# Attention transposes in three groups under a pinned TensorE order, the last token group of layer 1 issued later, and one norm pass on ScalarE

## The chip, the cores and the metric

The kernel runs on one core of one Trainium2 chip. The metric is the device time of one execution in microseconds (us). Engines are named as the profile names them: PE is TensorE's matmul stream and PEld its weight loads, DVE is VectorE, ACT is ScalarE, POOL is GpSimd, SP is SyncE. The program holds one list of instructions for each engine, and engines wait for each other by semaphores.

## The reference

One inference step of a two-layer backbone over 128 context tokens and 1024 latent tokens, width 1024, all in float32. Layer 0 mixes tokens by chunkwise retention and pooling, layer 1 by attention; each is followed by a SwiGLU FFN, with RMS norms around every part and a shift and scale from a conditioning vector. Cut to what the change touches:

```python
def rmsnorm(x, gain):
    y = x32 * lax.rsqrt(jnp.mean(x32 * x32, axis=-1, keepdims=True) + EPS)
    return y.astype(x.dtype) * gain

# attention of the latent tokens: 8 heads, 2 key/value heads, head dimension 128,
# keys: 256 cached and 1024 latent ones
s = jnp.einsum('bqkgd,btkd->bkgqt', qblk, k).astype(jnp.float32) * scale
p = jax.nn.softmax(s, axis=-1).astype(v.dtype)
return jnp.einsum('bkgqt,btkd->bqkgd', p, v)

xs = xs + g2s * rmsnorm(fs, norm_gain[i, 3])              # end of layer i
hs = rmsnorm(xs, norm_gain[i, 0]) * (1.0 + sc1s) + sh1s   # start of the next
```

## The kernel before, in words

All nine token tiles of 128 (tile 0 is the context, 1 to 8 the latent tokens) stay in SBUF. A float32 product is made of three passes in a faster 32-bit format: `split` writes the high half of a tile by a ScalarE cast (L156) and the low half by a VectorE subtraction (L157), and `mm3` (L179) multiplies high by high, high by low and low by high.

**Order of the work.** The kernel is traced in Python. A scheduler then sets the order on each engine by its own estimate of when each instruction is ready; the order of the Python program is its priority, not its law. Two calls bind it: `keep_in_program_order` ties an instruction behind the one traced before it on its engine, and `issue_after` puts a block behind a named instruction. In the kernel before, TensorE's attention work is bound by neither. The framework sets the semaphores, one for each pair of instructions that touch the same data.

**Attention** (L1256 to L1362) goes over 32 pairs n, each of one latent token tile and two heads (e = 0 and 1).
- `q_split` (L1256 on) splits the queries of pair n on GpSimd.
- `scores(n, e)` multiplies 128 queries by 1280 keys into PSUM columns 1280·e to 1280·e+1280 in three pieces of 512, 512 and 256 columns, each of three matmuls. The kernel counts PSUM in banks of 512 columns (`bank`), so that both heads' quarter pieces of 256 lie in bank 2: columns 1024 to 1280 are head 0's last piece, 1280 to 1536 are head 1's first. Then come the row maximum over 1280 columns on VectorE (L1271), the exponential with its sum on ScalarE (L1273), the reciprocal (L1274), and the scaling by it, on ScalarE for e = 0 (L1278) and on VectorE for e = 1 (L1276).
- `p_trans(n, u)`, written T, makes four 128x128 transposes on TensorE (L1289), two key blocks of both heads, into PSUM bank 5 or 6, and splits the result (L156, L157).
- `values(n, u)`, written V, multiplies two key blocks of the values by the transposed probabilities: six matmuls of 256 columns, summed over u = 0 to 4 in bank 7. After u = 4 ScalarE copies the result out (L1307).

The order of a pair is written as a string (L1343): T, V and v stand for `p_trans` and `values` of pair n and of the pair before, S0 and S1 for `scores` of the next pair. At eight of the pairs a block of `w_o` is loaded and split as well (L1356 to L1359).

**From layer 0 to layer 1.** The FFN's output stage of layer 0 (`output`) ends every token tile with `chain_steps`: a gated norm (L220 to L234), the residual sum stored to DRAM (L235), the sum of squares on ScalarE (L237), its power -1/2 on GpSimd (L184, L185), and the normalised tile (L240, VectorE). When three tiles are through, `hsteps` queues eight steps in the list `later`; each makes three transposes (L255), shift and scale on ScalarE (L258), and the high and low half on VectorE (L260, L261). `go(n)` issues the next n of them. The projection of layer 1 runs `qkv_step` for blocks bi = 0 and 1 over token groups g = 0, 1, 2 of three tiles, 24 matmuls each, with calls of `go` between.

Of the kernel before, what the change touches and what calls it, by code (L numbers as in the profile page):

```python
# [64 lines left out]
def hybrid_step_kernel(ctx: ExitStack, tc: tile.TileContext, a: dict, outs: list):  # L65
# [45 lines left out]
    def bank(i, n=1):  # L111
        return PS[:, i * 512:(i + n) * 512]
# [25 lines left out]
    def tok(t):  # L138
        return O[:, :, t * 128:(t + 1) * 128]
# [28 lines left out]
    def load_pair(src, hl):  # L168
        hi, lo = hl
        for s in range(2):  # L170
            load_unit(src[:, 4 * s:4 * s + 4], (hi[:, 4 * s:4 * s + 4].rearrange("p k f -> p (k f)"),
                                               lo[:, 4 * s:4 * s + 4].rearrange("p k f -> p (k f)")), k=4)

    def mm3(out, items, first=True, last=True):
        n = 3 * len(items)
        c = 0
        for lh, ll, rh, rl in items:
            for x, y in ((lh, rh), (lh, rl), (ll, rh)):
                nc.tensor.matmul(out=out, lhsT=x, rhs=y, start=(first and c == 0), stop=(last and c == n - 1))  # L179
                c += 1  # L180

    def rstd_of(ss, n, w=1):
# [23 lines left out]
    def load_gates(l, s):  # L206
        for k in range(2):
            nc.sync.dma_start(out=GB[k], in_=g_scr[l][s][k][0:1, :].broadcast_to([128, D]))

    def chain_steps(t, src, xs, xd, junk, last=False):  # L210
        if last:
            xb = (XB + [RAW[:, 0], RAW[:, 1]])[t % 4]
        else:
            xb = XB[t] if t < 2 else (XB[0], GB[0], XB[1])[(t - 2) % 3]
        nc.sync.dma_start(out=xb, in_=xs)
        ot = tok(t)
        ss = sm()
        if len(src.shape) == 2:
            src = src.rearrange("p (k f) -> p k f", k=KD)
        nc.scalar.activation(junk, src, ACTF.Square, accum_out=ss)  # L220
        r = rstd_of(ss, D)
        yield
        g = GB[0 if t == 0 else 1].rearrange("p (k f) -> p k f", k=KD)
        x3 = xb.rearrange("p (k f) -> p k f", k=KD)
        if last:
            n = 2 if t == 8 else 1
            for i in range(n):
                c = slice(i * KD // n, (i + 1) * KD // n)
                nc.vector.scalar_tensor_tensor(ot[:, c], src[:, c], r, g[:, c], op0=ALU.mult, op1=ALU.mult)  # L229
                nc.vector.tensor_add(x3[:, c], ot[:, c], x3[:, c])  # L230
                nc.sync.dma_start(out=xd.rearrange("t (k f) -> t k f", k=KD)[:, c], in_=x3[:, c])
            return
        nc.vector.scalar_tensor_tensor(ot, src, r, g, op0=ALU.mult, op1=ALU.mult)
        nc.vector.tensor_add(x3, ot, x3)  # L234
        nc.gpsimd.dma_start(out=xd, in_=xb)  # L235
        s2 = sm()
        nc.scalar.activation(ot, x3, ACTF.Square, accum_out=s2)  # L237
        r2 = rstd_of(s2, D)
        yield
        nc.vector.tensor_scalar(ot, x3, r2, None, op0=ALU.mult)  # L240

    def chain(*args, **kw):
        for _ in chain_steps(*args, **kw):
# [21 lines left out]
    def go(n=99):  # L265
        for _ in range(min(n, len(later))):
            later.pop(0)()
# [497 lines left out]
    class FFN:  # L765
# [241 lines left out]
        def output(self):  # L1007
            l = self.l
            last_layer = self.next_sub is None
            self.S2 = open_mid2(F32)  # L1010
            self.out_load(3)
            self.out_load(4)
            if l == 0:
                nc.gpsimd.memset(XGT[:, 2048:3072], 0.0)
                adaq.append(Ada(1, 2, ada_bufs(XGT[:, 0:4096]), 4))
            f0, nb = 0, 0
            live = []

            def advance():
                for item in list(live):  # L1020
                    t, g = item
                    if next(g, None) is None and g.gi_frame is None:
                        live.remove(item)
                        if not last_layer and t % 3 == 2:
                            hsteps(t // 3, self.next_sub, (6, 7) if t < 8 else (4, 5), t == 8)

            for ci, nf in enumerate(NCH):
                fs = range(f0, f0 + nf)
                f0 += nf
                todo = list(range(f0, f0 + NCH[ci + 1])) if ci + 1 < len(NCH) else []  # L1030
                start = 6 if ci == 0 else 3
                every = (18 - start) // len(todo) if todo else 99
                lastc = ci == len(NCH) - 1
                if lastc:
                    load_gates(l, 1)
                    if not last_layer:
                        load_blk(0)
                for t in range(NT):
                    js = slice(t * 128, t * 128 + 128)
                    for half in range(2):  # L1040
                        ps = bank(nb % 4)
                        items = []
                        for f in fs:
                            gh, gl, wh, wl = self.out_slot(f)
                            items.append((gh[:, js], gl[:, js], wh[half], wl[half]))
                        mm3(ps, items)
                        dst = O[:, 4 * half:4 * half + 4, js]
                        p3 = ps.rearrange("p (k f) -> p k f", k=4)
                        if ci == 0:
                            nc.scalar.copy(dst, p3)  # L1050
                        else:
                            nc.vector.tensor_add(dst, p3, dst)  # L1052
                        nb += 1
                        n = 2 * t + half
                        if todo and n >= start and (n - start) % every == 0:
                            f = todo.pop(0)
                            self.out_split(f)
                            if f + 3 < NF:
                                self.out_load(f + 3)
                        if not lastc and ci > 0 and n % 4 == 3:  # L1060
                            hook()
                        go(2)
                    if lastc:
                        advance()
                        junk = PS[:, 2048:3072].rearrange("p (k f) -> p k f", k=KD)
                        g = chain_steps(t, tok(t), self.xs(t), self.xd(t), junk, last=last_layer)
                        next(g)
                        live.append((t, g))
            while live:
                advance()  # L1070
                if not last_layer and live and live[-1][0] == 8:
                    go()
            if not last_layer:
                load_blk(1)
# [181 lines left out]
    def q_split(n):  # L1256
        t, hp = pairs[n]
        qh, ql = qsb[n % 2]
        src = O[:, 2 * hp:2 * hp + 2, t * 128:(t + 1) * 128]
        nc.gpsimd.tensor_copy(qh, src)  # L1260
        nc.gpsimd.tensor_sub(ql, src, qh)
# [19 lines left out]
    pts = {}  # L1281

    def p_trans(n, u):
        tp = bank(5 + u % 2)
        for jj in range(2):
            for e in range(2):
                c = (2 * jj + e) * 128
                j = 2 * u + jj
                nc.tensor.transpose(tp[:, c:c + 128], smx[n, e][:, j * 128:(j + 1) * 128], ident)  # L1289
        b = RR[:, 1024 * (st["u"] % 6):1024 * (st["u"] % 6) + 1024]  # L1290
        st["u"] += 1
        split(b[:, 0:512], b[:, 512:1024], tp)
        pts[n, u] = b
# [15 lines left out]
    for g in range(NG):  # L1309
        for bi in range(2):  # L1310
            for t in range(3 * g, 3 * g + 3):
                qkv_step(bi, t)
                go(2 if (g, bi) > (0, 0) else 0)
        go()
    load_blk(2)
    load_blk(3)
    side = {(3, 2): cached_k, (5, 1): cached_v}
# [19 lines left out]
        f()  # L1337

    q_split(1)
    for n in range(len(pairs)):  # L1340
        if n + 2 < len(pairs):
            q_split(n + 2)
        for w in 'T0 v3 S0 T1 v4 T2 S1 T3 V0 V1 T4 V2'.split():  # L1343
            c, u = w[0], int(w[1])
            if c == 'S' and n + 1 < len(pairs):
                scores(n + 1, u)
            elif c == 'T':
                p_trans(n, u)
            elif c == 'V':
                values(n, u)  # L1350
            elif c == 'v' and n:
                values(n - 1, u)
        if n % 2 == 1 and 6 <= n // 2 < 14:
            k = n // 2 - 6
            r = raw()
            nc.sync.dma_start(out=r, in_=a["w_o"][0, k * 128:(k + 1) * 128, :])  # L1356
            with tc.issue_after(st["act"].ins if hasattr(st["act"], "ins") else st["act"]):
                nc.scalar.copy(units[k][0], r)
            nc.vector.tensor_sub(units[k][1], r, units[k][0])  # L1359

    values(len(pairs) - 1, 3)
    values(len(pairs) - 1, 4)  # L1362
    load_gates(1, 0)
    F = FFN(1, M1, lambda t: x_scr[2][t], x_out, None)
    out_proj(F, units, [0, 1, 2, 3, 4, 5, 6, 7], [0, 1, 2, 3, 4], lambda t: [(tok(t), 0, 8)],
# [31 lines left out]
```

## Time and profile before

| | |
|---|---|
| median of 3 runs | 2904.22 us (2900.73 to 2904.52) |
| the profiled execution's own time | 2904.19 us |
| its span, first to last instruction | 2902.4 us |
| PE busy | 2835.7 us, 98% of the span |
| DVE, ACT, POOL busy | 1796.5, 1044.0, 299.8 us |
| mean granted TensorE clock | 0.994 |
| attention, first to last transpose (L1289) | 1699.6 to 2003.5 us |

The page of the profile lists busy time by engine, the span in 40 slices, the queues, the chain that ended last and the costliest groups of instructions. A row of the timeline reads: start and length in us, engine, line, operation, tile written <- tiles read, shapes, count of instructions merged, and in brackets the engine's idle time before it and what ended it. In attention the tiles tell the steps apart: `PS<-CT,XGT` at L1289 are transposes; `PS<-MID1True,RR` at L179 are scores (keys in MID1True), 128x512 for the large pieces and 128x256 for the quarter pieces; `PS<-RR` and `PS<-RR,MID2True` are values. The table by windows gives busy us of each engine, the count of instructions in brackets, and PEclk, the granted share of the TensorE clock.

### The profile page before, as it was taken

The numbers are of one execution on the slowest core, as the hardware profiler recorded it, in microseconds if no ns is written. First come the engines' busy times: TensorE is split into PE (matmuls) and PEld (weight loads), VectorE is DVE, ScalarE is ACT, GpSimd is POOL, SyncE is SP. The second block draws the span as 40 slices with busy tenths as digits, with TensorE's granted clock in tenths as the row PEclk, the third lists the DMA queues.
The fourth block names the chain that finished last, engine by engine and source line by source line (L and its number), as shares of the span: only waits on it lengthen the run. The fifth ranks groups of instructions, "written<-read, shape, count | busy, mean of one in ns | idle before, by whom it ended". The sixth has DMA issues, their size and how long they took to land. (4 is left out here: it accounts for less than half of the span.)

```text
span 2902.4 us, 44728 instructions
## 1 busy us (share of the span) xinstructions
PE 2835.7 (98%) x17979; PEld 2554.2 (88%) x17979; DVE 1796.5 (62%) x3019; ACT 1044.0 (36%) x1950; POOL 299.8 (10%) x542
## 2 busy tenths in 40 slices
PE   7999999999999999999999999999999999999998
PEld 4889998788999999977779988888889999998886
DVE  5784455526767676665775667786486555554455
ACT  5222222426223223331243457785362222234111
POOL 2010111111000000000033621110100000000000
PEclk9999999999999999999999999999999999999999
DMA  7541110412333333353331000001223222225222
GB/s 247 163 122 52 36 34 26 141 65 73 105 114 120 112 126 99 129 167 115 122 132 62 23 16 1 23 30 59 91 81 111 72 73 77 76 74 180 78 92 102
DMA packets 194056, 262.59 MB, mean 90 GB/s; under 512 B 10220, under 2 KB 139688, under 8 KB 193720
## 3 DMA queue, kind: packets, MB, share of 16 engines
q1 hardware_dynamic: 182272, 217.88, 23.8%
q0 software_dynamic: 11088, 41.47, 3.8%
q8 instruction: 141, 2.31, 0.3%
q14 instruction: 67, 0.55, 0.1%
q10 hardware_dynamic: 488, 0.38, 0.0%
HBM read 213.52 MB, written 46.17 MB: 89 GB/s over the span
## 5 line engine op out<-in xcount | busy, mean ns | idle before, releaser
L179 PE MATMUL PS<-RR 128*128 128x256 f32 (+2 forms) x6270 | 1134.9, 333 | 1.3 <-ACT O L1050 0.7
L179 PEld LDWEIGHTS PS<-RR 128*128 128x128 f32 x6270 | 959.9, 190 | 117.6 <-issue 19.0
L843 PE MATMUL PS<-RR 128*128 128x288 f32 x5324 | 734.2, 297 | 12.9 <-ACT RR L156 7.0
L843 PEld LDWEIGHTS PS<-RR 128*128 128x128 f32 x5324 | 717.0, 189 | 24.2 <-ACT RR L156 7.9
L156 ACT CAST RR<-O 128x512 fp32r<-128x512 f32 (+1 forms) x242 | 151.8, 628 | 535.1 <-PE PS L843 468.7
L179 PE MATMUL PS<-RR,MID2True 128*128 128x256 f32 (+1 forms) x1416 | 269.2, 338 | 0.2 <-ACT RR L156 0.2
L1052 DVE TENSOR_TENSOR O<-PS,O 128x512 f32<-128x512 f32 x216 | 148.9, 689 | 172.8 <-PE PS L179 172.0
L179 PEld LDWEIGHTS PS<-RR,MID2True 128*128 128x128 f32 x1416 | 218.2, 189 | 30.5 <-ACT RR L156 0.8
L157 DVE TENSOR_TENSOR RR<-O,RR 128x512 fp32r<-128x512 f32 (+1 forms) x242 | 167.5, 693 | 72.4 <-ACT RR L156 72.4
L157 DVE TENSOR_TENSOR RR<-RAW,RR 128x512 fp32r<-128x512 f32 (+1 forms) x119 | 110.2, 932 | 101.8 <-ACT RR L156 78.7
L345 DVE SCALAR_TENSOR_TENSOR O<-O,PW 128x512 f32<-128x512 f32 x224 | 159.7, 745 | 18.4 <-ACT O L343 9.4
L156 ACT CAST RR<-RAW 128x512 fp32r<-128x512 f32 (+1 forms) x119 | 95.4, 808 | 207.4 <-PE PS L843 92.4
L179 PE MATMUL PS<-MID1True,RR 128*128 128x512 f32 (+1 forms) x630 | 166.7, 372 | 2.2 <-ACT XGT L1273 1.7
L843 PE MATMUL PS<-MID1True,RR 128*128 128x288 f32 x1100 | 159.9, 295 | 0.0
L843 PEld LDWEIGHTS PS<-MID1True,RR 128*128 128x128 f32 x1100 | 150.9, 189 | 0.0
L843 PE MATMUL PS<-MID2True,RR 128*128 128x288 f32 x968 | 147.0, 295 | 0.0
L184 POOL TENSOR_SCALAR SM<-SM 128x1 f32<-128x1 f32 (+1 forms) x153 | 56.6, 370 | 793.0 <-ACT PS L220 304.8
L843 PEld LDWEIGHTS PS<-MID2True,RR 128*128 128x128 f32 x968 | 135.5, 189 | 0.0
L874 POOL DMA_DIRECT2D gg<-XGT x44 | 23.6, 537 | 961.5 <-DVE XGT L873 961.5
L1271 DVE TENSOR_REDUCE SM<-PS 128x1 f32<-128x1280 f32 x64 | 95.5, 1491 | 40.5 <-PE PS L179 40.0
L179 PEld LDWEIGHTS PS<-MID1True,RR 128*128 128x128 f32 x630 | 102.7, 189 | 17.7 <-ACT XGT L1273 2.6
L156 ACT CAST RR<-PS 128x512 fp32r<-128x512 f32 x160 | 93.7, 587 | 64.6 <-PE PS L1289 63.5
(292 smaller groups left out, 3091.0 us busy)
## 6 DMA issues: line engine op xcount, KB each, us to landing
O<-in_w_ada_dram SPq DMA_DIRECT2D x64, 512.0 KB
RAW<-in_w_ffn_in_dram SPq DMA_DIRECT2D x100, 256.0 KB
gg<-XGT POOLq DMA_DIRECT2D x44, 576.0 KB, 3.1
O<-in_w_ffn_in_dram SPq DMA_DIRECT2D x92, 256.0 KB
RAW<-in_w_ffn_out_dram SPq DMA_DIRECT2D x30, 512.0 KB
MID2False<-gg SPq DMA_DIRECT2D x26, 576.0 KB
RAW<-in_w_in_even_dram SPq DMA_DIRECT2D x28, 512.0 KB
x<-XGT POOLq DMA_DIRECT2D x27, 512.0 KB, 3.2
```

What stands on the lines that cost most here:

```text
L156: nc.scalar.copy(hi, src)
L157: nc.vector.tensor_sub(lo, src, hi)
L179: nc.tensor.matmul(out=out, lhsT=x, rhs=y, start=(first and c == 0), stop=(last and c == n - 1))
L184: nc.gpsimd.tensor_scalar(r, ss, 1.0 / n, EPS, op0=ALU.mult, op1=ALU.add)
L345: nc.vector.scalar_tensor_tensor(self.acc[kind], b[:, k], sv, self.acc[kind], op0=ALU.mult, op1=ALU.add)
L843: nc.tensor.matmul(out=ps, lhsT=u[:, ks], rhs=v, start=first and n == 0, stop=n == 11, skip_group_check=not first)
L874: nc.gpsimd.dma_start(out=gg_scr[self.l][f], in_=XGT[:, 2880:4032])
L1052: nc.vector.tensor_add(dst, p3, dst)
L1271: nc.vector.reduce_max(nm, sp, axis=AX.X, negate=True)
```

## The change

Three edits.

1. **Attention order.** The string becomes `T0 T1 v3 S0 v4 S1 T2 T3 V0 V1 T4 V2`, so that a pair's five transpose steps stand in groups of two, two and one. From the first pair to the end of the last, every TensorE instruction of `mm3` and `p_trans` is bound to the program's order by `keep_in_program_order`. The bank of `p_trans` alternates over all steps, not within a pair.
2. **Last token group of layer 1.** The eight steps of group g = 2, which wait in `later` when the projection begins, are issued from g = 1 on, not within g = 0.
3. **Norm pass.** In the FFN's output stage of layer 0 the last step of `chain_steps` (the normalised tile, nine times) runs on ScalarE.

```diff
+    pin = {"pe": False}
+
+    def pe(ins):
+        return tc.keep_in_program_order(ins) if pin["pe"] else ins
...
-                nc.tensor.matmul(out=out, lhsT=x, rhs=y, start=(first and c == 0), stop=(last and c == n - 1))
+                pe(nc.tensor.matmul(out=out, lhsT=x, rhs=y, start=(first and c == 0), stop=(last and c == n - 1)))
...
-        nc.vector.tensor_scalar(ot, x3, r2, None, op0=ALU.mult)
+        if act:
+            nc.scalar.activation(ot, x3, ACTF.Identity, scale=r2)
+        else:
+            nc.vector.tensor_scalar(ot, x3, r2, None, op0=ALU.mult)
...
-                        g = chain_steps(t, tok(t), self.xs(t), self.xd(t), junk, last=last_layer)
+                        g = chain_steps(t, tok(t), self.xs(t), self.xd(t), junk, last=last_layer, act=True)
...
     def p_trans(n, u):
-        tp = bank(5 + u % 2)
+        tp = bank(5 + st["u"] % 2)
...
-                nc.tensor.transpose(tp[:, c:c + 128], smx[n, e][:, j * 128:(j + 1) * 128], ident)
+                pe(nc.tensor.transpose(tp[:, c:c + 128], smx[n, e][:, j * 128:(j + 1) * 128], ident))
...
-                go(2 if (g, bi) > (0, 0) else 0)
-        go()
+                go(2 if g else 0)
+        if g:
+            go()
...
     q_split(1)
+    pin["pe"] = True
...
-        for w in 'T0 v3 S0 T1 v4 T2 S1 T3 V0 V1 T4 V2'.split():
+        for w in 'T0 T1 v3 S0 v4 S1 T2 T3 V0 V1 T4 V2'.split():
...
     values(len(pairs) - 1, 4)
+    pin["pe"] = False
```

More of the change, by code (lines that the diff above doesn't have):

```diff
@@ L208, in load_gates, with chain_steps @@
             nc.sync.dma_start(out=GB[k], in_=g_scr[l][s][k][0:1, :].broadcast_to([128, D]))
-    def chain_steps(t, src, xs, xd, junk, last=False):
+    def chain_steps(t, src, xs, xd, junk, last=False, act=False):
         if last:
```

## The prediction

> **What bounds the kernel now.** I read the page first, then the timeline of one attention pair by engine, then the granted clock by windows, and last the passage from layer 0 to layer 1.
>
> ```profile
> span 2902.4 us, 44728 instructions
> ## 1 busy us (share of the span) xinstructions
> PE 2835.7 (98%) x17979; PEld 2554.2 (88%) x17979; DVE 1796.5 (62%) x3019; ACT 1044.0 (36%) x1950; POOL 299.8 (10%) x542
> ```
>
> TensorE is busy for 98% of 2902.4 us. Whatever makes it idle is paid in full, and whatever another engine saves is worth nothing unless TensorE was waiting for it. So I ask of each edit only where TensorE will stand still. Most depends on the 32 attention pairs. One of them on TensorE:
>
> ```profile
> 1856.43 0.61 PE L179 MATMUL PS<-MID1True,RR 128*128 128x256 f32 x3
> 1856.87 0.60 PE L1289 MATMUL PS<-CT,XGT 128*128 128x128 f32 x4
> 1857.23 0.95 PE L179 MATMUL PS<-RR,MID2True 128*128 128x256 f32 x6
> 1858.02 1.55 PE L179 MATMUL PS<-MID1True,RR 128*128 128x512 f32 x6
> 1859.41 0.73 PE L1289 MATMUL PS<-CT,XGT 128*128 128x128 f32 x5
> 1860.07 0.62 PE L179 MATMUL PS<-MID1True,RR 128*128 128x256 f32 x3
> ```
>
> Lengths overlap, since matmuls are pipelined, so I take differences of starts. A transpose step and a values step together need 1858.02 - 1856.87 = 1.15 us. Six large score matmuls need 1859.41 - 1858.02 = 1.39. A matmul of 256 columns needs 0.12 (47 of them stand at 5.88 us in a row below), so a values step is 0.72, a transpose step 0.43, and three quarter-piece matmuls 0.36. A head's scores are 1.39 + 0.36 = 1.75. A pair is 5 x 1.15 + 2 x 1.75 = 9.25 us of TensorE. The same pair on VectorE and on ScalarE:
>
> ```profile
> 1857.07 1.49 DVE L1271 TENSOR_REDUCE SM<-PS 128x1 f32<-128x1280 f32 x1
> 1858.48 1.28 DVE L157 TENSOR_TENSOR RR<-PS,RR 128x512 fp32r<-128x512 f32 x2
> 1860.05 0.16 DVE L1274 RECIPROCAL SM<-SM 128x1 f32<-128x1 f32 x1 [0.29 <-ACT XGT L1273]
> 1860.73 1.49 DVE L1271 TENSOR_REDUCE SM<-PS 128x1 f32<-128x1280 f32 x1 [0.52 <-PE PS L179]
> 1862.14 1.28 DVE L157 TENSOR_TENSOR RR<-PS,RR 128x512 fp32r<-128x512 f32 x2
> 1863.72 0.16 DVE L1274 RECIPROCAL SM<-SM 128x1 f32<-128x1 f32 x1 [0.31 <-ACT XGT L1273]
> 1863.92 0.89 DVE L1276 TENSOR_SCALAR XGT<-XGT,SM 128x1280 f32<-128x1280 f32 x1
> 1864.73 0.68 DVE L157 TENSOR_TENSOR RR<-PS,RR 128x512 fp32r<-128x512 f32 x1
> 1866.59 1.49 DVE L1271 TENSOR_REDUCE SM<-PS 128x1 f32<-128x1280 f32 x1 [1.19 <-PE PS L179]
> ```
>
> ```profile
> 1858.60 1.33 ACT L1273 ACTIVATE XGT<-PS,SM 128x1280 f32<-128x1280 f32 x1
> 1859.83 0.19 ACT L1273 ACTIVATION_READ_ACCUMULATOR XGT<-PS,SM 128x1 f32 x1
> ```
>
> Head 0's row maximum starts at 1857.07 and the next pair's at 1866.59, so a pair now takes 9.52 us: TensorE stands still for 0.27 of it. The place is the last row of the TensorE view. Head 1's quarter piece starts at 1860.07, 0.05 after ScalarE's exponential of head 0 ended (1859.83 + 0.19 = 1860.02). The two touch different columns, 1280 to 1536 and 0 to 1280, but share bank 2. An earlier pair has the releaser by name:
>
> ```profile
> 1707.95 0.42 PEld L179 LDWEIGHTS PS<-MID1True,RR 128*128 128x128 f32 x3 [0.21 <-ACT XGT L1273]
> ```
>
> So a bank that is being read holds up a write to its other columns. The scheduler has arranged the present order around that: head 1's six large matmuls (1858.02), which touch banks 3 and 4, go first although the program traces the quarter piece first, then five transposes, and the quarter piece last. The 3.6 us that head 0's maximum and exponential take are filled with transposes, values and scores.
>
> **Part 1, the attention order.** The binding forbids that arrangement. TensorE must now take the string literally: scores of head 0, v4, then scores of head 1 beginning with the quarter piece, which waits for head 0's exponential. Everything behind it in TensorE's list waits too: head 1's six large matmuls, T2, T3, V0 and all that follows. Nothing else is left to fill with, since the other TensorE work nearby, the output projection, needs the results of attention. I follow one pair, from the start of head 0's quarter piece:
>
> - To the start of head 1's quarter piece: 1860.07 - 1856.43 = 3.64 us (three matmuls, maximum, exponential). TensorE has 0.36 + 0.72 (v4) = 1.08 of it to do and idles for 2.56.
> - Head 1's scores: 1.75. The maximum follows 0.28 after their last start slot (1857.07 - 1856.43 less 0.36): 2.03.
> - Maximum, exponential, reciprocal and scaling of head 1: from 1860.73 to 1863.92 + 0.89 = 1864.81, that is 4.08, and 0.05 until TensorE goes on: 4.13. T0 of the next pair needs this. Between, TensorE has T2, T3, V0, V1, T4, V2: 3 x 0.43 + 3 x 0.72 = 3.45 us, against 0.28 + 4.13 = 4.41. It idles for 0.96.
> - T0, T1, v3 and six large matmuls of head 0: 0.86 + 0.72 + 1.39 = 2.97.
>
> The sum is 3.64 + 2.03 + 4.13 + 2.97 = 12.77 us, which is 9.25 of work plus 2.56 and 0.96 of idling. Against 9.52 that is 3.25 more. There are 32 pairs, and 31 rounds hold scores: 31 x 3.25 = 101 us.
>
> What the edit gains is inside this sum already. The new bank rule lets T0 follow T4 of the pair before in another bank, and the 0.27 of idling is what it could win at most, 8 us in all. I cost the grouping of transposes itself at nothing: in the TensorE view transposes and matmuls follow each other with no gap in either direction. VectorE and ScalarE do the same work as now in a longer pair, so I let them be in time; if they are not, that is a rival below. The first round (no v3, v4) and the last (no scores) differ by under 1 us each way, and I leave them out.
>
> Then the clock. The windows below are chosen at the times at which the granted clock changes, 3.41 us each:
>
> ```profile
> 1518.71:1522.12 3.41, 1.31 (x12) 1.07 (x10) 2.68 (x7) 1.68 (x4) 2.10 (x3) 1.00 0.33 135
> 1522.12:1525.53 3.41, 2.76 (x12) 2.67 (x13) 3.32 (x5) 0.67 (x1) 0.00 (x0) 0.50 0.58 156
> ...
> 1535.77:1539.18 3.41, 1.95 (x16) 1.56 (x14) 2.06 (x8) 2.13 (x7) 0.89 (x2) 1.00 0.00 0
> 1539.18:1542.59 3.41, 2.61 (x23) 2.41 (x22) 2.96 (x8) 0.67 (x1) 0.74 (x1) 1.00 0.00 0
> 2146.77:2150.18 3.41, 1.80 (x11) 1.57 (x12) 3.41 (x8) 1.16 (x3) 0.00 (x0) 1.00 0.00 0
> 2150.18:2153.59 3.41, 3.35 (x15) 3.00 (x13) 3.41 (x9) 1.53 (x4) 0.00 (x0) 0.50 0.02 5
> ```
>
> A window with 1.31 or 1.80 us of PE work is followed by one at clock 0.50; one with 1.95 is not. So about 1.6 us of idling within one window costs half the clock in the next. An idle stretch of 2.56 puts 1.6 or more into one window unless a border cuts it near its middle, which is 0.66 of 3.41 us of possible places: four in five are followed by a slow window. That window can start from 0.95 us before head 1's scores to 1.80 after their start. Half clock costs those 1.75 us of work between 0 (the window starts as they end) and 1.7 (it starts with them), about 1.05 in the mean; what else falls into it has the 0.96 of idling as cover. 0.8 x 1.05 = 0.85 per pair, 31 x 0.85 = 26 us. The pair comes to 13.6 us. That is near four windows (13.65), so that the phase should move little from pair to pair.
>
> The Trainium skill ("TensorE: Matmul & The Clock Gate", section "HAM oscillation — how this bites in real kernels") gives as its rule that gaps of PE idling stay harmless up to about 3.4 us. By it 2.56 would cost no clock and these 26 us would fall away. The trace speaks against it: the window at 2146.77 had 1.80 us of work and the next one got 0.50 all the same.
>
> Part 1: 101 + 26 = 127 us.
>
> **Parts 2 and 3, at the start of layer 1.**
>
> ```profile
> 1513.92 5.88 PE L179 MATMUL PS<-RR 128*128 128x256 f32 x47
> 1519.64 0.38 PE L255 MATMUL PS<-CT,O 128*128 128x128 f32 x2
> 1522.77 1.12 PE L255 MATMUL PS<-CT,O 128*128 128x128 f32 x4 [2.74 <-DVE O L240]
> 1523.53 8.35 PE L179 MATMUL PS<-RR 128*128 128x256 f32 x47
> ```
>
> ```profile
> 1520.21 1.02 DVE L261 TENSOR_TENSOR RR<-XGT,RR 128x384 fp32r<-128x384 f32 x2
> 1521.96 0.75 DVE L240 TENSOR_SCALAR O<-XGT,SM 128x1024 f32<-128x1024 f32 x1 [0.73 <-POOL SM L185]
> 1522.63 2.35 DVE L157 TENSOR_TENSOR RR<-RAW,RR 128x1024 fp32r<-128x1024 f32 x2
> ```
>
> The third transpose of the group waits 2.74 us for tile 8's norm pass, and the 47 matmuls after it take 8.35 instead of 5.88 at the lowered clock: 5.2 us at most that the later issue can win. Those 47 are of block 1, whose low halves are split at 1522.63, behind the same norm pass. With that pass off VectorE the split can follow at 1521.23; if it stays there, the matmuls wait for it instead (its first half ends near 1522.4), and only some 0.3 us are won. If the scheduler draws it forward, nearly all 5.2 are. The moved steps issue no DMA; they go beside the 72 matmuls of g = 1, as they go beside g = 0 now.
>
> ```profile
> L237 ACT ACTIVATE O<-XGT x27: 1058/1060/1093, 564.2 to 2117.8; 128x1024 f32<-128x1024 f32 x27
> ```
>
> ScalarE has no such pass of 128x1024 yet; the nearest row is its square sum at 1.06 us, against 0.75 on VectorE. Nine passes at 0.3 more lie beside the output stage's matmuls. If the shift-and-scale steps (L258) queue behind them and transposes wait for those, it may cost up to 3 us. From -5 to +3 I take -2.
>
> **The sum.** 2904.19 for the profiled execution + 127 - 2 = 3029 us. It stands 0.03 from the median of the runs, so no further step is needed.
>
> **The rivals.**
> - *The clock holds.* The idling is there but costs no clock, as the page's rule has it. For it: 0.66 of 3.41 places escape in any case, and a steady phase could be one that escapes. Against: the two windows above. 2904 + 101 - 2 = 3003. Chance 0.13.
> - *VectorE's and ScalarE's order makes it worse.* T4's cast must queue with head 1's exponential, its subtraction with head 1's scaling (L1276, 0.89); T1 of the next pair needs T4's bank. A subtraction (0.68) placed ahead of the scaling lengthens the round by about 0.8: 13.6 + 0.8 = 14.4 us, 31 x 4.88 - 2 = +149, 3053. For it: nothing binds these two engines, and eight pairs carry the w_o split besides. Against, the busy us of TensorE, its weight loads, VectorE and ScalarE in a present pair with a w_o split:
>
> ```profile
> 1850.54:1860.07 9.53, 9.53 (x69) 8.53 (x69) 8.32 (x12) 8.01 (x13) 1.15 (x2) 1.00 0.19 55
> ```
>
> Each of the two would have some 5 us free in a pair of 13.6. Chance 0.16.
> - *No wait for the bank.* If head 1's quarter piece did not wait, T0's 0.96 would remain: 9.25 + 0.96 = 10.21, 31 x 0.69 - 2 = +19, 2923. Against: the 0.05 after the exponential. Chance 0.05.
> - *Faster.* The place is the same two waits: if both fell below 0.27 us together, the pair would run at TensorE's 9.25, and 31 x 0.27 + 2 = 10 us would be won: 2894. It needs head 1's probabilities 3.45 us after its scores, where the rows add to 4.41. Chance 0.03.
> - *The binding doesn't bind*, and the order stays as it is: 2902, no difference. It ties every TensorE instruction to the one before, so I give it 0.03.
>
> **How the numbers follow.** The forecast keeps 0.60 and is the likeliest: 3029. The range runs from the clock rival with parts 2 and 3 at their best (2904 + 101 - 5, rounded down to 2996) to the order rival at its worst with some lost clock more (3062), and leaves out the three cheap cases, 0.11 together, and the tails. About 0.2% (6 us) is what a measurement of this kernel can tell from no change. Faster by more than that is the fourth rival alone, 0.03; within it the fifth, 0.03; slower the rest, 0.94.
>
> **What would show it.**
>
> ```profile
> L1289 PE MATMUL PS<-CT,XGT x640: 270/272/332, 1699.6 to 2003.5; 128*128 128x128 f32 x160
> ```
>
> Right: transposes spread over some 430 us instead of 304; in each pair a score row 128x256 x3 on TensorE with about 2.5 us of idling released by ScalarE's L1273, with six 128x512 right behind it, and a transpose row with up to 1 us released by VectorE's L1276; PEclk at 8 or below in the attention slices; PE's share near 94%. Wrong: pairs of 10 us or less, or large matmuls still ahead of the quarter piece. For parts 2 and 3: nine L240 passes moved to ScalarE, and no transpose waiting 2.7 us near 1520.

## The result, and the profile after

3027.43 us median of 4 runs (3027.04 to 3028.44) against 2904.22: ratio 1.0426, 95% interval 1.0414 to 1.0439. The change is slower by 123 us.

The page of the changed kernel, where TensorE's share has fallen from 98% to 95%:

```profile
span 3026.7 us, 44724 instructions
## 1 busy us (share of the span) xinstructions
PE 2869.5 (95%) x17979; PEld 2572.7 (85%) x17979; DVE 1794.2 (59%) x3010; ACT 1060.8 (35%) x1959; POOL 297.9 (10%) x542
```

Two attention pairs in the timeline of TensorE (transposes are now L1297, `mm3` is L184, the exponential L1281, head 1's scaling L1284):

```profile
1851.15 1.92 PE L184 MATMUL PS<-MID1True,RR 128*128 128x512 f32 x9
1852.91 0.87 PE L184 MATMUL PS<-RR,MID2True 128*128 128x256 f32 x6
1856.11 2.01 PE L184 MATMUL PS<-MID1True,RR 128*128 128x256 f32 x9 [2.32 <-ACT XGT L1281]
...
1861.50 0.27 PE L1297 MATMUL PS<-CT,XGT 128*128 128x128 f32 x1
1862.27 1.25 PE L1297 MATMUL PS<-CT,XGT 128*128 128x128 f32 x7 [0.50 <-DVE XGT L1284]
1863.28 0.95 PE L184 MATMUL PS<-RR,MID2True 128*128 128x256 f32 x6
1864.07 1.92 PE L184 MATMUL PS<-MID1True,RR 128*128 128x512 f32 x9
1865.83 0.87 PE L184 MATMUL PS<-RR,MID2True 128*128 128x256 f32 x6
1869.03 3.47 PE L184 MATMUL PS<-MID1True,RR 128*128 128x256 f32 x9 [2.32 <-ACT XGT L1281]
1872.34 1.03 PE L1297 MATMUL PS<-CT,XGT 128*128 128x128 f32 x8
```

Read it against the pair of the kernel before that the prediction quotes. Head 0's nine score matmuls are in one row, v4 is the next, and then TensorE idles 2.32 us until ScalarE's exponential of head 0 is over. The row that waits begins with the quarter piece (its form is 128x256) and holds all nine matmuls of head 1. The second wait is that of T0: its first transpose, which needs head 0 alone, goes, and the next one waits for VectorE's scaling of head 1. A third, small one is hidden in that row of seven. It shows in the weight loads, which come just ahead of the transposes:

```profile
1862.27 0.31 PEld L1297 LDWEIGHTS PS<-CT,XGT 128*128 128x128 f32 x3 [0.73 <-DVE XGT L1284]
1862.87 0.42 PEld L1297 LDWEIGHTS PS<-CT,XGT 128*128 128x128 f32 x4 [0.29 <-DVE RR L157]
```

T0's last transpose starts at 1862.54 and T1's first at 1862.87, 0.33 us later, where 0.11 is a transpose's time. The other 0.22 is a wait for T4's bank, since VectorE's subtraction of T4 stands behind its scaling of head 1.

The same nine matmuls take 2.01 us in the first pair and 3.47 in the second. The clock explains that. As in the prediction, the windows are laid on its changes:

```profile
1851.78:1855.20 3.42, 2.00 (x14) 1.61 (x12) 1.66 (x2) 0.94 (x2) 0.00 (x0) 1.00 0.00 0
1855.20:1858.61 3.41, 2.50 (x16) 2.20 (x17) 0.62 (x2) 2.24 (x4) 0.58 (x2) 1.00 0.00 0
...
1865.44:1868.85 3.41, 1.26 (x10) 1.01 (x8) 1.49 (x1) 1.67 (x3) 0.00 (x0) 1.00 0.00 0
1868.85:1872.26 3.41, 3.23 (x9) 2.68 (x10) 0.16 (x1) 1.49 (x3) 0.02 (x1) 0.50 0.02 5
```

The first idle stretch is cut by a window border: 2.00 and 2.50 us of work remain on either side, and the clock stays. The second lies in one window, leaves 1.26 us of work in it, and the next window runs at 0.50. From head 0's maximum to the next pair's, pairs take 12.92 and 14.38 us in turn after the first (but for one of 15.14 near the end), 13.65 in the mean, which is four windows.

Where the 124.3 us between the two profiled spans lie, told by the starts of the same instructions: 2.4 are there already before the first changed instruction (run to run), -9.4 come between there and the first row maximum of attention, 130.4 between the first and the last row maximum (433.5 against 303.0 us), 0.8 behind it.

### The profile page after: what moved, and what is told of

Its sections match the earlier page's. It is cut to its first block, busy times and chain, and to the rows that moved or that the text cites. A ratio compares the mean times of both kernels' runs of the same rounds, so it can differ in the third digit from the quotient of the medians.

```text
span 3026.7 us, 44724 instructions
## 1 busy us (share of the span) xinstructions
PE 2869.5 (95%) x17979; PEld 2572.7 (85%) x17979; DVE 1794.2 (59%) x3010; ACT 1060.8 (35%) x1959; POOL 297.9 (10%) x542
## 5 line engine op out<-in xcount | busy, mean ns | idle before, releaser
L184 PE MATMUL PS<-RR 128*128 128x256 f32 (+2 forms) x6270 | 1130.2, 333 | 1.3 <-ACT O L1058 0.7
L184 PEld LDWEIGHTS PS<-RR 128*128 128x128 f32 x6270 | 956.6, 190 | 116.4 <-issue 19.1
L184 PE MATMUL PS<-RR,MID2True 128*128 128x256 f32 (+1 forms) x1416 | 274.3, 339 | 0.2
L184 PEld LDWEIGHTS PS<-RR,MID2True 128*128 128x128 f32 x1416 | 220.2, 189 | 30.6 <-DVE RR L157 0.8
L184 PE MATMUL PS<-MID1True,RR 128*128 128x512 f32 (+1 forms) x630 | 171.1, 411 | 74.0 <-ACT XGT L1281 73.5
L184 PEld LDWEIGHTS PS<-MID1True,RR 128*128 128x128 f32 x630 | 121.6, 219 | 100.9 <-ACT XGT L1281 80.3
L851 PEld LDWEIGHTS PS<-MID1True,RR 128*128 128x128 f32 x1100 | 150.9, 189 | 0.0
```

What stands on the lines that cost most here:

```text
L184: pe(nc.tensor.matmul(out=out, lhsT=x, rhs=y, start=(first and c == 0), stop=(last and c == n - 1)))
L851: nc.tensor.matmul(out=ps, lhsT=u[:, ks], rhs=v, start=first and n == 0, stop=n == 11, skip_group_check=not first)
```

## The experiments

All times below are medians, each with its ratio to the kernel before on the same chip. "Pair" is the interval between the row maxima of head 0 of successive pairs, in the profile. My theory was the prediction's: bound to the string, TensorE waits at head 1's quarter piece for a PSUM bank, and at T0 for head 1's probabilities, and the longer wait costs clock. The main rivals: the grouping of the transposes costs, binding costs in any order, or idling costs no clock.

**Nothing bound.**

```diff
     q_split(1)
-    pin["pe"] = True
```

> The changed kernel with nothing bound on TensorE; the new string, the alternating banks and parts 2 and 3 stay. Theory (the binding makes head 1's quarter piece wait for head 0's exponential): the scheduler again puts head 1's large matmuls and other work ahead of the quarter piece, a pair is back at 9.3 to 9.6 us, and the kernel at about 2895 us, before less the roughly 9 us that the start of layer 1 shows in the two traces. Rival (the grouping of the transposes itself costs, through banks 5 and 6 and the splits): above 3000 us, pairs above 12 us.

2908.27 us, 1.0018 (1.0009 to 1.0027). The binding carries nearly all of the loss: 119 us of the 133 that lie between the changed kernel and parts 2 and 3 alone, the next run below. The other 14 are the unbound new string's. Pairs alternate between 11.2 and 8.3 us, later 11.0 and 9.4. In TensorE's timeline a transpose now waits for a bank:

```profile
1857.08 0.66 PE L1297 MATMUL PS<-CT,XGT 128*128 128x128 f32 x4 [1.06 <-DVE RR L157]
```

So the rival of the grouping had a small share, a tenth of the loss, by the order that the scheduler makes of the new string.

**Parts 2 and 3 alone.** The kernel before with the later issue and the ScalarE pass, and no line of attention changed.

> The kernel before with parts 2 and 3 alone, attention untouched. Theory: the 9 us between the traces at the start of layer 1 belong to these parts: 2895 us. Rival (they come from the bound attention, whose early matmuls no longer stand between the projection's last steps): 2901 to 2904 us.

2894.27 us, 0.9972 (0.9960 to 0.9983), pairs at 9.51 to 9.54 after the first. The gain belongs to these parts.

**Quarter piece last.**

```diff
-        ... else ((0, 256), (256, 512), (768, 512))):
+        ... else ((256, 512), (768, 512), (0, 256))):
```

> The changed kernel, but head 1's scores are traced with the two large pieces first and the quarter piece last. Theory: 1.39 us of large matmuls now stand ahead of the waiting one, which wait shrinks from 2.56 to 1.17, too little for the clock to fall: pair 11.4 to 11.5 us, 31 x 2.15 less than the changed kernel's 13.65: 2961 us, no slow clock in the attention rounds. Rival (the wait is for data of head 0, not for its bank, or the grouping costs): no change, 3027 us.

2968.62 us, 1.0224 (1.0210 to 1.0238): 59 us less than the changed kernel by nothing but the order of three pieces in the trace. TensorE's timeline:

```profile
1853.20 0.88 PE L184 MATMUL PS<-RR,MID2True 128*128 128x256 f32 x6
1853.91 1.56 PE L184 MATMUL PS<-MID1True,RR 128*128 128x512 f32 x6
1856.39 0.62 PE L184 MATMUL PS<-MID1True,RR 128*128 128x256 f32 x3 [0.93 <-ACT XGT L1281]
```

The large pieces run while the exponential does, and only the quarter piece waits. The wait falls from 2.32 us to 0.93, by 1.39, which is the six matmuls' length. Pairs take 11.75 and none is followed by a slow clock after the first round. I had 11.4 to 11.5; the wait ahead of T0 grew by 0.2 us (0.72 against 0.50).

**Filling the wait.**

```diff
+            elif c == 'D' and n + 1 < len(pairs):
+                qh = qsb[(n + 1) % 2][0]
+                for k in range(9):
+                    pe(nc.tensor.matmul(out=bank(5 + st["u"] % 2)[:, 0:256], lhsT=qh[:, 0],
+                                        rhs=KR[:, 0, 0, 0:256], start=True, stop=True))
...
-        for w in 'T0 T1 v3 S0 v4 S1 T2 T3 V0 V1 T4 V2'.split():
+        for w in 'T0 T1 v3 S0 D0 v4 S1 T2 T3 V0 V1 T4 V2'.split():
```

> The changed kernel with nine matmuls of 256 columns added between S0 and v4 of each pair, into the transpose bank that is free there; their result is overwritten unused. Theory: they lie in the wait for head 0's exponential, which stays as long, but idling falls from 2.3 to about 1.2 us by the trace's own measure, so that the clock holds: every pair takes the 12.92 us that every second one takes now instead of 12.92 and 14.38 in turn; 31 x 0.73 = 23 us less: 3005 us with 279 matmuls more. Rival (idling of 2.3 us costs no clock, the longer pairs have another cause): 3027 us or, if the matmuls aren't hidden, up to 31 x 1.08 more, 3060.

3005.70 us, 1.0353 (1.0339 to 1.0367). 279 useless matmuls make the changed kernel 21.7 us faster. Their row is the second here:

```profile
1851.17 1.92 PE L184 MATMUL PS<-MID1True,RR 128*128 128x512 f32 x9
1852.93 1.23 PE L1360 MATMUL PS<-MID1True,RR 128*128 128x256 f32 x9
1854.00 0.87 PE L184 MATMUL PS<-RR,MID2True 128*128 128x256 f32 x6
1856.13 2.01 PE L184 MATMUL PS<-MID1True,RR 128*128 128x256 f32 x9 [1.26 <-ACT XGT L1281]
```

Head 1's scores start 4.96 us after head 0's, as without them (1851.15 to 1856.11): the wait is the same, only part of it is spent working. After the first, every pair takes 12.91 to 12.97 us, and the clock stays at 1.00 from the second round to the last. So the clock's share of the loss is about 22 us, and the rival that idling of 2.3 us is free falls.

**The old string, bound.**

```diff
-        for w in 'T0 T1 v3 S0 v4 S1 T2 T3 V0 V1 T4 V2'.split():
+        for w in 'T0 v3 S0 T1 v4 T2 S1 T3 V0 V1 T4 V2'.split():
```

> The changed kernel with the string of the kernel before, bound. Theory: binding alone does most of the harm: T1, v4 and T2 (1.58 us) lie between S0 and S1, so TensorE idles 1.70 there and 1.39 ahead of T0: pair 12.5 us, 31 x 2.97 above parts 2 and 3 alone: about 2986 us; the idling is near the 1.6 us from which the clock falls, so up to 20 us more. Rival (the grouping in the new string costs, binding doesn't): 2894 to 2910 us.

2981.89 us, 1.0273 (1.0259 to 1.0287), pairs 12.20 to 12.23 (but for the first two and one of 12.38). Both waits are there, shorter or longer by the work that now lies between:

```profile
1850.80 2.02 PE L184 MATMUL PS<-MID1True,RR 128*128 128x256 f32 x9 [1.45 <-ACT XGT L1281]
...
1856.98 0.55 PE L1297 MATMUL PS<-CT,XGT 128*128 128x128 f32 x3 [1.03 <-DVE XGT L1284]
```

After the first rounds the clock stays: an idle stretch of 1.45 costs none. Bound, the old string is 88 us slower than parts 2 and 3 alone; unbound it is level with them (the last run of this section).

**Part 2 alone** (the later issue of the last token group):

> The kernel before with the later issue of the last token group alone. Theory: it removes the 2.74 us wait for tile 8's norm pass and the slow clock behind it, 5.2 us in all, unless block 1's low halves stay where they are on VectorE: 2898 to 2903 us. Rival (the 9 us of parts 2 and 3 come from the norm pass on ScalarE): no difference, 2903 to 2904 us, with a wait in the same place.

2901.11 us, 0.9992 (0.9983 to 1.0001): no difference that can be told for certain. The wait stayed:

```profile
1525.26 0.66 PE L255 MATMUL PS<-CT,O 128*128 128x128 f32 x4 [2.63 <-DVE O L240]
1526.39 10.15 PE L179 MATMUL PS<-RR 128*128 128x256 f32 x70 [0.48 <-DVE RR L157]
```

The scheduler still put the group's first transposes ahead of block 1, and block 1 waited 0.48 more for its low half behind the same VectorE pass.

**Part 3 alone** (the norm pass on ScalarE):

> The kernel before with the norm pass on ScalarE alone. Theory: VectorE no longer stands still for GpSimd's power ahead of each norm pass (0.7 to 2.2 us each), the output stage's last tiles finish earlier, and the 1.72 us wait of the transposes with its slow clock goes; the 2.74 us wait stays but shorter: 3 to 5 us less, 2899 us. Rival (part 2 brings all of it): 2903 us.

2898.90 us, 0.9986 (0.9977 to 0.9995). VectorE's timeline in the output stage, first before, then with part 3 alone:

```profile
1471.07 1.28 DVE L233 SCALAR_TENSOR_TENSOR O<-O,SM,XGT 128x1024 f32<-128x1024 f32 x1 [0.71 <-POOL SM L185]
...
1476.23 0.75 DVE L240 TENSOR_SCALAR O<-XGT,SM 128x1024 f32<-128x1024 f32 x1 [1.54 <-POOL SM L185]
1477.70 1.28 DVE L233 SCALAR_TENSOR_TENSOR O<-O,SM,XGT 128x1024 f32<-128x1024 f32 x1 [0.71 <-POOL SM L185]
```

```profile
1469.43 1.28 DVE L233 SCALAR_TENSOR_TENSOR O<-O,SM,XGT 128x1024 f32<-128x1024 f32 x1 [2.56 <-POOL SM L185]
...
1475.61 1.28 DVE L233 SCALAR_TENSOR_TENSOR O<-O,SM,XGT 128x1024 f32<-128x1024 f32 x1 [2.56 <-POOL SM L185]
```

A tile's chain took 6.63 us (1471.07 to 1477.70), now 6.18. TensorE's matmuls of a tile take 5.54 (1474.14 to 1479.68 in the kernel before), so the chain had been falling behind them, and still does, by less. The pass itself is longer on ScalarE, 1.15 us against 0.75. VectorE still waits for GpSimd, once for 2.56 us where it waited twice, 0.71 and 1.54; of the 0.75 that its list is shorter by, 0.45 a tile came out as gain. Both of TensorE's waits that lowered the clock are gone: the one of 1.72 us near 1490 and the one of 2.74 near 1520; two others, of 1.44 and 1.72, appear at 1507 and 1512 and leave it alone. Together the two parts win 9.2 us, alone 2.3 and 4.5. That they win more together isn't clear of noise: by its interval the 9.2 may be 4.9 to 11.6. The trace of both does show that with part 3 the pass of tile 8 is no longer in part 2's way: 111 matmuls run on from 1516.34 without a wait.

**A bank of its own for each head.**

```diff
-            mm3(PS[:, 1280 * e + c0:1280 * e + c0 + w],
+            mm3(PS[:, 1536 * e + c0:1536 * e + c0 + w],
...
-        tp = bank(5 + st["u"] % 2)
+        tp = bank(6 + st["u"] % 2)
...
-        op = bank(7)[:, 0:256]
+        op = PS[:, 1280:1536]
...
-        for w in 'T0 T1 v3 S0 v4 S1 T2 T3 V0 V1 T4 V2'.split():
+        for w in 'T0 T1 v3 v4 S0 S1 T2 T3 V0 V1 T4 V2'.split():
```

> The changed kernel with head 1's scores moved to PSUM columns 1536 to 2816, so that the heads share no bank; transposes use banks 6 and 7, values the second half of bank 2, and v4 goes ahead of S0 (order T0 T1 v3 v4 S0 S1 T2 T3 V0 V1 T4 V2, bound). Theory (the bank is what head 1's scores wait for): S1 follows S0 at once; what is left is the 0.96 us until the next pair's probabilities are ready, part of it moved to V0, which now waits for head 0's exponential in bank 2: pair 10.2 to 10.4 us, about 2919 us, no slow clock in the attention rounds. Rival (head 1 needs head 0's exponential for another reason, or the bound order is slow as such): a wait of over 2 us stays in front of S1, above 3000 us.

3022.04 us, 1.0411 (1.0396 to 1.0425): a miss by 100 us, and the picture of neither theory nor rival. The timeline, all engines:

```profile
1852.64 0.98 PE L184 MATMUL PS<-RR 128*128 128x256 f32 x6 [0.48 <-ACT XGT L1281]
...
1854.22 1.33 ACT L1281 ACTIVATE XGT<-PS,SM 128x1280 f32<-128x1280 f32 x1
...
1855.53 1.07 ACT L156 CAST RR<-PS 128x512 fp32r<-128x512 f32 x2
...
1856.67 1.28 DVE L157 TENSOR_TENSOR RR<-PS,RR 128x512 fp32r<-128x512 f32 x2
...
1857.41 1.97 PE L1297 MATMUL PS<-CT,XGT 128*128 128x128 f32 x8 [1.94 <-DVE RR L157]
...
1861.34 3.66 PE L184 MATMUL PS<-MID1True,RR 128*128 128x512 f32 x18
```

What the theory says of the bank holds: all eighteen score matmuls of both heads run in one row, with no wait between. And the wait went where the bank went: the values now share bank 2 with head 0's scores, and V0, the first row, waits 0.48 us for head 0's exponential. But T0 now waits 1.94 us for T3's bank. T3's transposes were done at about 1852.2; their cast stands in ScalarE's list behind head 1's exponential and ends near 1856.1, and the subtraction follows. Added to the wait, the clock falls as before (pairs of 12.28 without it and 13.7 to 13.8 with it).

**The same with T2 and T3 ahead of S1.**

```diff
-        for w in 'T0 T1 v3 v4 S0 S1 T2 T3 V0 V1 T4 V2'.split():
+        for w in 'T0 T1 v3 v4 S0 T2 T3 S1 V0 V1 T4 V2'.split():
```

> The kernel with a bank of its own for each head, with T2 and T3 ahead of S1 (order T0 T1 v3 v4 S0 T2 T3 S1 V0 V1 T4 V2, bound). Theory (the 1.94 us ahead of T0 in the run before came from T3's cast, which stood behind head 1's exponential in ScalarE's list, so that T3's bank came free late): T3's cast is now done before head 0's exponential; that wait goes, and the one for the probabilities is left: 2.59 us of work after S1 against 4.41, 1.82 of idling, pair 11.1 to 11.3 us, about 2946 us, up to 20 more if the clock falls. Rival (T0 waits for something else): no change, 3022 us.

2973.07 us, 1.0239 (1.0225 to 1.0254), pairs 11.96 against 12.28 to 13.8. The wait for T3's bank is gone, so the cause was the right one. The price wasn't: 2946 was expected. TensorE's timeline:

```profile
1851.69 0.66 PE L1297 MATMUL PS<-CT,XGT 128*128 128x128 f32 x4 [1.01 <-ACT XGT L1286]
1852.90 0.65 PE L1297 MATMUL PS<-CT,XGT 128*128 128x128 f32 x4 [0.55 <-DVE RR L157]
```

T0 waits for head 0's scaling (L1286), which ScalarE's list now has behind head 1's exponential, and T1 for T4's bank.

**An order made from the sums**, with the quarter pieces traced apart from the large ones, on all three parts:

```diff
-    def scores(n, e):
+    def scores(n, e, part):
...
-        for c0, w in (((0, 512), (512, 512), (1024, 256)) if e == 0 else ((0, 256), (256, 512), (768, 512))):
+        for c0, w in (((0, 512), (512, 512)), ((256, 512), (768, 512)))[e] if part == 0 else (((1024, 256),), ((0, 256),))[e]:
...
+        if part == 0:
+            return
...
-        for w in 'T0 T1 v3 S0 v4 S1 T2 T3 V0 V1 T4 V2'.split():
+        for w in 'T0 s0 S1 v3 T1 v4 s1 T2 T3 V0 V1 N0 T4 V2'.split():
```

> All of the change with another bound order, made from the theory's sums: each head's scores are traced in two parts, the two large pieces and the quarter piece, and the string is T0 s0 S1 v3 T1 v4 s1 T2 T3 V0 V1 N0 T4 V2 (S1 and s1 head 1's large and quarter pieces of the next pair, s0 head 0's quarter piece, N0 the large pieces of head 0 of the pair after that). Theory: between the quarter pieces lie 1.39 + 0.72 + 0.43 + 0.72 = 3.26 us of work against the 3.28 that head 0's maximum and exponential take after the first; between s1 and T0 lie 3.45 + 1.39 = 4.84 against 4.41: TensorE hardly idles, pair 9.25 to 9.40 us, 31 x 0.15 to 0.28 below parts 2 and 3 alone: 2886 to 2890 us. Rival (binding TensorE is slow whatever the order, since the other engines' lists don't follow): 2900 us or more.

2917.39 us, 1.0050 (1.0036 to 1.0064), pairs 10.07. Neither of the changed kernel's two large waits is left, but T3 waits for T1's bank, since T1's cast came behind head 0's exponential on ScalarE. The weight loads of T3 show it:

```profile
1854.52 0.42 PEld L1299 LDWEIGHTS PS<-CT,XGT 128*128 128x128 f32 x4 [0.38 <-DVE RR L157]
```

With T1 directly behind `s0` instead (`T0 s0 T1 S1 v3 v4 s1 T2 T3 V0 V1 N0 T4 V2`):

> The ordered kernel with T1 directly behind head 0's quarter piece (T0 s0 T1 S1 v3 v4 s1 T2 T3 V0 V1 N0 T4 V2, bound). In the run before, a pair took 10.07 us: T1's cast stood behind head 0's exponential on ScalarE, its subtraction came late, and T3 waited for that bank. Theory: T1's cast is now done before that exponential starts, T2 and T3 find their banks free, and a pair takes 9.25 to 9.5 us: 2887 to 2894 us, level with parts 2 and 3 alone or up to 7 us under. Rival (three engines' lists can't be kept in step by binding one of them; another late cast or subtraction takes over): pairs of 9.8 us or more, above 2902 us.

2911.63 us, 1.0023 (1.0015 to 1.0032), pairs 9.91. Again a list of another engine decides; TensorE's timeline shows the next wait in line:

```profile
1851.54 1.04 PE L1299 MATMUL PS<-CT,XGT 128*128 128x128 f32 x8
1852.87 0.98 PE L184 MATMUL PS<-RR 128*128 128x256 f32 x6 [0.30 <-ACT O L1317]
```

Here V0 waits until ScalarE has copied out the pair before, a copy that stands behind head 0's scaling. Both rivals named for these two runs were right: the order that TensorE's sums asked for is no gain with ScalarE's and VectorE's lists left as they fall.

**The old string, unbound, with parts 2 and 3 and the alternating banks:**

> Parts 2 and 3 and the alternating banks for the transposes, with the old string and nothing bound. Theory: the unbound new string lost 14 us against parts 2 and 3 alone by its order, not by the banks; so this is at 2894 us or some 2 us under it (0.06 us per pair of waiting for a transpose bank falls away). Rival (the alternating banks cost it): 2900 to 2908 us.

2896.04 us, 0.9973 (0.9962 to 0.9985): level with parts 2 and 3 alone. The banks are not what costs in the unbound new string, and they win nothing.

The fastest version is parts 2 and 3 alone, 2894.27 us.

## Why the prediction was right

It had 3029 (2996 to 3062); 3027.43 was measured. By its own steps:

- *The bank wait.* Right in place, order and size. Bound, head 1's quarter piece goes first and waits: from v4's end (1852.91 + 0.72) to 1856.11 are 2.48 us, forecast 2.56. That it is the bank is shown from three sides: with the quarter piece last the wait shrinks by the length of what may pass, with a bank of its own it is gone, and V0, put into head 0's bank, waits there for head 0's exponential. The rows name ScalarE's semaphore as what ends the wait, though the two touch different columns. So the program's semaphores go by the bank here, and not only by the data touched. Whether the chip itself would hold up such a write no run shows.
- *The wait ahead of T0.* Right in place; 0.66 by the starts (1862.27 - 1861.50, less a transpose's 0.11), forecast 0.96. I had not seen that T0's first transpose needs head 0 alone, nor the 0.22 that T1 waits behind it.
- *The pair.* 12.92 at full clock, forecast 12.77. Closer than its terms: the two foreseen waits came out 0.38 smaller, T1's wait of 0.22 was not foreseen, and what is left, 12.92 - 2.48 - 0.66 - 0.22 = 9.56, is 0.31 more than the 9.25 of work in the sum. Where in the round these 0.31 lie I have not settled.
- *The clock.* The term was 26 us and its measure is about 22 (the filled kernel). Its make-up was another: not four pairs in five at 1.05 us, but every second pair at 1.46 (14.38 - 12.92). Two pairs fill eight windows, so that idle stretches meet the same two places of the grid each time; one is cut by a border and the other isn't. That "the phase should move little" was half right: it moves 0.73 us (14.38 - 13.65) forth and back, and these two places should have replaced the mean over all.
- *The edge of 1.6 us.* It was drawn from too few windows. Laid over all fourteen traces, every one of the 124 windows at full clock with at most 1.50 us of PE busy time was followed by one at 0.50; of 34 with 1.51 to 1.80 six were; of those with more none was. The window of 1.80 at 2146.77 was one of the six; one of 1.51, in the run with a bank for each head, was not. So a slow window was certain only where about 1.9 us or more of one window were idle. With 1.9 the prediction's own way of counting gives some 0.64 of the places, not four in five.
- *The Trainium skill's rule* ("TensorE: Matmul & The Clock Gate", section "HAM oscillation — how this bites in real kernels"), gaps harmless up to about 3.4 us of idling, doesn't hold here. The measured stretches of 2.3 us cost half the clock for 3.41 us when one window held enough of them (1.26 us of work left), and stretches of 1.45 cost nothing.
- *First and last rounds.* "Under 1 us each way" held for the first: it takes 4.5 us more than before (18.0 against 13.5), a later pair 4.15 in the mean. It did not hold for the last, where head 1's maximum follows head 0's 1.4 us later than before (5.05 against 3.66). The measured 130.4 stands 3.4 above the forecast 127: 1.4 from there, 0.4 from the first round, and 0.05 in each of the other thirty.
- *Parts 2 and 3.* Wrong in size: -2, from -5 to +3, against -9.2 measured alone. The failing step is "nine passes at 0.3 more lie beside the output stage's matmuls": I priced the pass itself and not the place in VectorE's list that it gives up. VectorE stood still for GpSimd's power ahead of each pass, 1.54 us at four tiles and 0.7 to 2.2 at the others, and the tiles' chain took 6.63 us a tile against TensorE's 5.54. Of TensorE's two long waits at the layer's end, 2.74 us were for the pass itself; the 1.72 ended with a ScalarE step that stands behind a square sum of that chain. That the shorter chain is what won the time is read from these rows and not tested apart. The row with the 1.54 was in the trace; I took only the last tile's.
- *The order of ScalarE and VectorE*, a rival at 0.16, came true in the changed kernel only in small: the wait of T1 for T4's bank, which it names, is there, but at 0.22 us and not 0.8. In four of the experiments it decided.
- *The range.* Its lower end is given as 2904 + 101 - 5, which is 3000 and not 2996. Nothing hangs on it.

So the errors, +3.4 in attention, -7.4 at the start of layer 1 and +2.4 from run to run, nearly cancelled. That the median came within 2 us is luck; that it fell near the middle of the range is not. One sign I named was wrong as well: PEclk at 8 or below in the attention slices. They read 9, since only one window in eight is slow (mean clock 0.94 from 1710 to 2110 us).

## What to carry to other kernels

Before an engine's order is bound by hand, write down for each instruction which PSUM bank it writes and who reads that bank last: the wait is for the bank, and everything behind it in the list waits along. Binding one engine of a chain of three moves the stall into the other two's lists, so compare with the unbound order first. An instruction that waits at the head of a list also costs what stands behind it. Moving it to another engine can pay even where it takes longer there (1.15 us against 0.75 for the norm pass), but not by its whole length and wait: here 0.45 us a tile.

## What the runs showed of the hardware that I had not expected

A round and the clock's windows can fall into step: a round of 12.92 us at full clock settled at 13.65, four windows of 3.41, by being slowed every second time. And work for nothing can pay: nine matmuls added to each of 31 rounds took 21.7 us off. TensorE's idle stretch fell from 2.32 to 1.26 us, and the clock held.
